# Four score stages of a chunked recurrence in two tensor runs instead of four

## The chip, the cores and the metric

The kernel runs on one core of a Trainium2 chip. The metric is device time in microseconds (us), the median of three executions; beside it stands one profiled execution, whose trace gives the durations below. In the rows, PE is TensorE (PEld its weight loads, PEq its sequencer), DVE is VectorE, ACT is ScalarE, POOL is GpSimd, SP is SyncE, whose queue issues the DMAs here.

## The reference

One layer over 2048 positions of width 1024. One input projection feeds three causal mixers that read the same input; their outputs are gated, concatenated, projected, added to the input and normalized:

```python
h = jnp.einsum('bsd,de->bse', x, w_in)
y_a = _sgu_mixer(a_u, a_v, ...) * silu(a_g)       # A: gMLP, chunks of 128
y_b = _conv_module(b_val, b_glu, ...) * silu(b_g) # B: causal depthwise conv, width 31
y_c = _hgrn2_mixer(c_q, c_f, c_i, lb, ...) * silu(c_g)
y = concat([y_a, y_b, y_c]) @ w_out
return _layernorm(DEEPNORM_ALPHA * x + y, ...)
```

The change is in C, four heads of width 128. With f the forget gate, k = 1 - f, q = silu(c_q) and b the running sum of log f inside a chunk, it needs, for positions t >= s of one chunk,

```python
scores[t, s] = sum_d q[t, d] * k[s, d] * exp(b[t, d] - b[s, d])
o_intra = scores @ v
```

and adds what the state of earlier chunks gives.

## The kernel before, in words

The sequence is worked in two halves of two groups of 512 positions. In each half come branch B, then (first half) A, then the values of C, then C; in the second half A follows C, and the output product ends the program. Each projection (proj_f) is 24 matmuls of 128x512: eight slices of the width, three matmuls each (L201 to L203), since weights and inputs are split into a high part (ACT, L147) and a low part (DVE, L148).

**One unit** of C (hgrn_unit) is one head h on one group g: 16 units. Its PE work is three projections (pm_f, pm_q, pm_cg) and, between their matmuls, short runs of small matmuls. The products of f inside a chunk of 128 are built in levels of 4: T holds the products of f over 1, 4 and 16 positions (T1 is f itself), X the queries and partial queries multiplied by them, K the keys. Four score stages follow each other: stage(0) for pairs inside 4 positions, stage(1) for 16, stage(2) for 64, and chunk_halves for the two halves of 128. Each is one run of matmuls into a bank named sc: 16 of 32x80, 16 of 32x48 (K in pieces of 32 columns), 8 of 64x96 and 4 of 64x64 (pieces of 64 columns). DVE then takes the valid entries over with copy_predicated, into S32 for the first two stages and into ST for the third, and ACT copies S32 onto the diagonal of ST (L433). Behind its matmuls each stage makes the next level: X (L457, L458), T (L469 to L472) and, in place, K (L475, L477); prep (L384 to L389) completes X ahead of a stage.

After the last stage DVE raises K and Q once more (L504, L505), PE transposes K (pk, L515), ACT copies the transposes, PE makes the state increments (pst, L531), DVE chains the states (L539), PE makes the outputs (po, L551 and L555), ACT squares them (jk, L560), POOL takes the inverse root (crs, L228), ACT scales (os, L565), PE transposes back (pt, L573), DVE gates (sg, L575), and SP stores. Branch B's normalization (bt, bb, bhn) runs late and lies partly among the units of C.

**Order.** Every projection slice calls tick(0.64), which advances a clock in the program and emits what is due; later(d, fn) queues a step d units ahead. The delays stand in line 47: stage 0 is due 4.5 after the unit's q projection, the next ones 5.5 after each other, then 2.5, 2.0, 2.5 and 6.0 to transposes, states, outputs and finish. On PE the small runs are pinned to the place in which they are emitted, among the projection matmuls of the same and the next unit. On the other engines a scheduler settles the order when the program is built, and every engine runs its own list strictly in that order.

**Buffers.** X, X4, X16 and Q64 have one buffer each, K and f two; PSUM has 8 banks: three mm for projections, two sc, one each of o (po), st (pst) and tr (pk, pt); B's transposes borrow o, st and tr.

Of the kernel before, what the change touches and what calls it, by code (L numbers as in the profile page):

```python
# [11 lines left out]
F32 = mybir.dt.float32  # L12
# [3 lines left out]
AF = mybir.ActivationFunctionType  # L16
# [30 lines left out]
DST0, DST, DKT, DPST, DPO, DPT = 4.5, 5.5, 2.5, 2.0, 2.5, 6.0  # L47
# [37 lines left out]
def _body(tc, nc, d, ctx):  # L85
# [271 lines left out]
    def hgrn_unit(h, g, gi, w, x, pl, vh, ST, S32):  # L357
        nm = f"{h}_{g}"
        wf_, wq, wg = w
        pf = proj_f(wf_, x, f"f{nm}")  # L360
        f = pl.tile([P, G], F32, tag="f", bufs=2, name=f"f{nm}")
        nc.scalar.activation(f, pf, AF.Sigmoid)
        K = pl.tile([P, G], F32, tag="K", bufs=2, name=f"K{nm}")
        nc.vector.tensor_scalar(f, f, oml[:, h : h + 1], lb[:, h : h + 1], ALU.mult, ALU.add)
        nc.vector.tensor_scalar(K, f, -1.0, 1.0, ALU.mult, ALU.add)

        pq = proj_f(wq, x, f"q{nm}")
        X1 = pl.tile([P, P, 11], F32, tag="X1", bufs=1, name=f"X1{nm}")
        nc.scalar.activation(X1[:, :, 7:11], pq.rearrange("p (n j) -> p n j", j=4), AF.Silu)
        f3 = f.rearrange("p (n j) -> p n j", j=4)  # L370
        nc.vector.tensor_mul(X1[:, :, 0:2], X1[:, :, 7:9], f3[:, :, 0:2])
        nc.vector.tensor_mul(X1[:, :, 4:7:2], X1[:, :, 9:11], f3[:, :, 2:4])

        cur = {"X": X1.rearrange("p n (s b) -> p n s b", b=1), "T": f3}
# [16 lines left out]
        def stage(st):
            b = 4 ** st
            n = G // (4 * b)
            nsc = 10 if st == 0 else 6
            X, T = cur["X"], cur["T"]
            pc = bank("sc", 2, f"sc{nm}_{st}")
            if st < 2:
                npar = 32 // (4 * b)
                w_ = nsc * b * npar
                pcv = pc[:, : 4 * w_].rearrange("p (c w) -> p c w", c=4)  # L400
                for c in range(4):
                    for r in range(4):
                        lo_ = c * P + 32 * r
                        p0 = lo_ // (4 * b)
                        pinned(nc.tensor.matmul(pcv[32 * r : 32 * r + 32, c, :], K[:, lo_ : lo_ + 32],
                                         X[:, p0 : p0 + npar, 1 : 1 + nsc, :],
                                         start=True, stop=True))
# [22 lines left out]
                if st == 1:  # L430
                    for r in range(4):
                        rr = slice(32 * r, 32 * r + 32)
                        nc.scalar.copy(ST[rr, :, rr], S32[rr])  # L433
            else:
                w_ = nsc * b
                pcv = pc[:, : 4 * w_].rearrange("p (c w) -> p c w", c=4)
                for c in range(4):
                    for m in range(2):
                        lo_ = c * P + 64 * m
                        pinned(nc.tensor.matmul(pcv[64 * m : 64 * m + 64, c, :], K[:, lo_ : lo_ + 64],  # L440
                                         X[:, lo_ // 64, 1:7, :], start=True, stop=True))
                for i, (j0, s0, nj) in enumerate(((1, 0, 3), (2, 3, 2), (3, 5, 1))):
                    mo, mw = MOFF[6 + i]
                    for m in range(2):
                        rr = slice(64 * m, 64 * m + 64)
                        nc.vector.copy_predicated(  # L446
                            ST[rr, :, 64 * m + j0 * b : 64 * m + (j0 + nj) * b],
                            msk[rr, mo : mo + mw].unsqueeze(1).to_broadcast([64, 4, mw]),
                            pcv[rr, :, s0 * b : (s0 + nj) * b])

            if st < 2:
                nb = 4 * b
                Xn = pl.tile([P, n // 4, 7, nb], F32, tag=f"X{nb}", bufs=1, name=f"X{nb}_{nm}")
                Xj = X.rearrange("p (m k) s b -> p m k s b", k=4)
                Tj = T.rearrange("p (m k) j -> p m k j", k=4)
                for k0, sl in ((0, slice(0, 2)), (2, slice(4, 7, 2))):
                    nc.vector.tensor_copy(Xn[:, :, sl, 0:b], Xj[:, :, k0 : k0 + 2, 0, :])  # L457
                    nc.vector.tensor_mul(  # L458
                        Xn[:, :, sl, b : 4 * b],
                        Xj[:, :, k0 : k0 + 2, 1:4, :].rearrange("p m k s b -> p m k (s b)"),  # L460
                        Tj[:, :, k0 : k0 + 2, 0:1].to_broadcast([P, n // 4, 2, 3 * b]))
            else:
                Xn = pl.tile([P, n, 64], F32, tag="Q64", bufs=1, name=f"Q64_{nm}")
                nc.vector.tensor_copy(Xn[:, :, 0:b], X[:, :, 0, :])
                nc.vector.tensor_mul(
                    Xn[:, :, b : 4 * b],
                    X[:, :, 1:4, :].rearrange("p n s b -> p n (s b)"),
                    T[:, :, 0:1].to_broadcast([P, n, 3 * b]))
            nc.vector.tensor_mul(T[:, :, 2], T[:, :, 2], T[:, :, 3])  # L469
            nc.vector.tensor_mul(T[:, :, 1], T[:, :, 1], T[:, :, 2])  # L470
            Tn = pl.tile([P, n], F32, tag=f"T{4 * b}", bufs=2, name=f"T{4 * b}_{nm}")
            nc.vector.tensor_mul(Tn, T[:, :, 0], T[:, :, 1])  # L472
# [12 lines left out]
            if st < 2:
                prep(st + 1)
                later(DST, lambda: stage(st + 1))
            else:
                later(DST, chunk_halves)

        def chunk_halves():
            X, T = cur["X"], cur["T"]

            Q = X.rearrange("p (c a) t -> p c a t", a=2)
            K4 = K.rearrange("p (c a t) -> p c a t", a=2, t=64)
            pc = bank("sc", 2, f"sc{nm}_3")
            pcv = pc[:, : 2 * 64].rearrange("p (c w) -> p c w", c=2)
            for c in range(4):
                e = 64 * (c % 2)
                pinned(nc.tensor.matmul(pcv[e : e + 64, c // 2, :], K4[:, c, 0, :], Q[:, c, 1, :],  # L500
                                        start=True, stop=True))
# [3 lines left out]
            nc.vector.tensor_mul(K4[:, :, 0, :], K4[:, :, 0, :], T[:, :, 1:2].to_broadcast([P, 4, 64]))  # L505
# [75 lines left out]
        later(DST0, lambda: stage(0))  # L581
# [211 lines left out]
    def free_c(gi, ft):  # L793
# [75 lines left out]
    stiles.append(pool("stiles", stack=es, side="right"))  # L869
# [181 lines left out]
```

## Time and profile before

| | |
|---|---|
| median of 3 executions | 927.51 us (927.38 to 928.24) |
| the profiled execution's own time | 927.59 us |
| its span, first to last instruction | 925.8 us |
| granted TensorE clock, mean | 0.994 |
| PE busy | 904.1 us (98%) |
| PEld / DVE / ACT / POOL busy | 738.2 / 713.8 / 392.2 / 81.2 us |
| C in the trace, first half | from 200.8 us (first pm_f) |
| first and last score matmul (sc) | 217.2 and 707.1 us |

A group's row gives the source line, engine, operation, out<-in, count, busy time and mean ns of one, then idle time of the engine before them and who ended it. A timeline row gives start and duration in us. The recorded duration of a matmul reaches to its result; the next one starts earlier, so distances between starts, not durations, tell what a matmul costs PE. The trace records two passes for each matmul of C's short runs, so that 16 matmuls read "x32".

### The profile page before, as it was taken

The numbers are of one execution on the slowest core, as the hardware profiler recorded it, in microseconds if no ns is written. First come the engines' busy times: TensorE is split into PE (matmuls) and PEld (weight loads), VectorE is DVE, ScalarE is ACT, GpSimd is POOL, SyncE is SP. The second block draws the span as 40 slices with busy tenths as digits, with TensorE's granted clock in tenths as the row PEclk, the third lists the DMA queues.
The fourth block names the chain that finished last, engine by engine and source line by source line (L and its number), as shares of the span: only waits on it lengthen the run. The fifth ranks groups of instructions, "written<-read, shape, count | busy, mean of one in ns | idle before, by whom it ended". The sixth has DMA issues, their size and how long they took to land.

```text
span 925.8 us, 15037 instructions
## 1 busy us (share of the span) xinstructions
PE 904.1 (98%) x5673; PEld 738.2 (80%) x5673; DVE 713.8 (77%) x1614; ACT 392.2 (42%) x774; POOL 81.2 (9%) x127
## 2 busy tenths in 40 slices
PE   9999998899999999999999999999999999999996
PEld 6889886787777887888888887887889888888885
DVE  5998899935688768997999777778786135898777
ACT  6624355143435336644314334444553343543450
POOL 0001200100010000001000000001012000221122
PEclk9999999899999999999999999999999999999999
DMA  7506786120102103421202011111151498455322
GB/s 259 185 25 224 257 297 248 55 91 24 46 35 69 47 13 110 147 91 64 66 3 92 24 68 36 57 36 58 36 182 58 156 347 292 160 182 183 135 92 91
DMA packets 60808, 107.43 MB, mean 116 GB/s; under 512 B 5312, under 2 KB 21952, under 8 KB 60608
## 3 DMA queue, kind: packets, MB, share of 16 engines
q1 hardware_dynamic: 60736, 106.48, 33.7%
q8 instruction: 44, 0.72, 0.3%
q14 instruction: 28, 0.23, 0.1%
HBM read 75.00 MB, written 31.46 MB: 115 GB/s over the span
## 4 chain that ended last, share of the span: by engine, by line
PE 74%; DVE 13%; DMA 4%; issue 3%; ACT 3%; POOL 2%; SPq 0%; POOLq 0%; DVEq 0%; ACTq 0%
DVE acc L285 5%; PE pm_q L201 3%; PE poz L201 3%; PE poz L203 3%; PE poz L202 3%; PE pm_q L203 3%; PE pm_q L202 3%; PE pm_f L201 3%; PE pm_ci L201 3%; PE pm_ci L203 3%; PE pm_ci L202 3%; PE pm_cg L201 3%; PE pm_f L203 3%; PE pm_f L202 3%; PE pm_cg L202 2%
## 5 line engine op out<-in xcount | busy, mean ns | idle before, releaser
L285 DVE SCALAR_TENSOR_TENSOR acc<-bh,vec,acc 128x512 f32<-128x512 f32 x240 | 172.3, 753 | 2.6
L148 DVE TENSOR_TENSOR wl<-rw,wh 128x512 fp32r<-128x512 f32 x84 | 57.0, 690 | 27.3 <-ACT wh L147 27.1
L147 ACT CAST wh<-rw 128x512 fp32r<-128x512 f32 x84 | 49.9, 618 | 40.7 <-PE pm_f L202 11.1
L201 PE MATMUL pm_f<-xhix,wh 128*128 128x512 f32 x96 | 41.1, 429 | 0.0
L201 PE MATMUL pm_q<-xhix,wh 128*128 128x512 f32 x96 | 40.6, 423 | 0.0
L560 ACT ACTIVATE jk<-po 128x128 f32<-128x128 f32 x64 | 17.7, 277 | 51.9 <-PE po L555 50.9
L201 PE MATMUL pm_cg<-xhix,wh 128*128 128x512 f32 x96 | 39.0, 406 | 0.0
L203 PE MATMUL pm_f<-xhix,wl 128*128 128x512 f32 x96 | 37.7, 393 | 0.0
L202 PE MATMUL pm_q<-xlox,wh 128*128 128x512 f32 x96 | 37.7, 392 | 0.0
L203 PE MATMUL pm_q<-xhix,wl 128*128 128x512 f32 x96 | 37.7, 392 | 0.0
L202 PE MATMUL pm_f<-xlox,wh 128*128 128x512 f32 x96 | 37.6, 392 | 0.0
L203 PE MATMUL pm_cg<-xhix,wl 128*128 128x512 f32 x96 | 37.5, 391 | 0.0
L202 PE MATMUL pm_cg<-xlox,wh 128*128 128x512 f32 x96 | 37.5, 391 | 0.0
L201 PE MATMUL pm_ci<-wh_ci,xhix 128*128 128x512 f32 x96 | 37.4, 389 | 0.0
L203 PE MATMUL pm_ci<-wh_ci,xlox 128*128 128x512 f32 x96 | 37.4, 389 | 0.0
L202 PE MATMUL pm_ci<-wl_ci,xhix 128*128 128x512 f32 x96 | 37.4, 389 | 0.0
L227 POOL TENSOR_SCALAR crs<-ss 128x4 f32<-128x4 f32 x16 | 3.3, 205 | 367.6 <-ACT jk L560 367.6
L355 ACT COPY vh<-pm_ci 128x512 f32<-128x512 f32 x16 | 9.4, 588 | 58.9 <-PE pm_ci L203 58.9
L446 DVE COPY_PREDICATED ST<-msk,sc 64x192 f32<-64x192 int32 (+2 forms) x96 | 28.8, 300 | 5.4 <-PE sc L440 3.1
L503 ACT COPY ST<-sc 64x128 f32<-64x128 f32 x32 | 8.3, 260 | 50.9 <-PE sc L500 50.7
L565 ACT ACTIVATE os<-po,crs 128x128 f32<-128x128 f32 x64 | 18.3, 368 | 24.6 <-POOL crs L228 24.6
L201 PE MATMUL pm_av<-wh_av,xhix 128*128 128x256 f32 x96 | 28.2, 293 | 0.0
(355 smaller groups left out, 2753.1 us busy)
## 6 DMA issues: line engine op xcount, KB each, us to landing
rw<-wf SPq DMA_DIRECT2D x84, 256.0 KB, 3.2
wob<-wo_dr SPq DMA_DIRECT2D x14, 1024.0 KB, 11.5
xr<-x SPq DMA_DIRECT2D x16, 512.0 KB, 3.8
ry<-y_dr SPq DMA_DIRECT2D x32, 256.0 KB, 2.8
out<-xr SPq DMA_DIRECT2D x15, 512.0 KB, 2.6
wo_dr<-wsh SPq DMA_DIRECT2D x28, 256.0 KB, 3.2
wo_dr<-wsl SPq DMA_DIRECT2D x28, 256.0 KB, 2.9
rx<-xT SPq DMA_DIRECT2D x24, 256.0 KB, 3.4
```

What stands on the lines that cost most here:

```text
L147: nc.scalar.copy(hi, src)
L148: nc.vector.tensor_sub(lo, src, hi.bitcast(F32))
L201: nc.tensor.matmul(out, wh, xh, start=first, stop=False, **kw)
L202: nc.tensor.matmul(out, wh, xl, start=False, stop=False, **kw)
L203: nc.tensor.matmul(out, wl, xh, start=False, stop=last, **kw)
L227: nc.gpsimd.tensor_scalar(r, mv_var, scale, EPS, ALU.mult, ALU.add)
L285: nc.vector.scalar_tensor_tensor(a, h[:, k : k + G], vcol(cw + k), a, ALU.mult, ALU.add)
L355: nc.scalar.copy(vh[:, gi * 4 + tt, :], pt)
L446: nc.vector.copy_predicated(ST[rr, :, 64 * m + j0 * b : 64 * m + (j0 + nj) * b], msk[rr, mo : mo + mw].unsqueeze(1).to_broadcast([64, 4, mw]),
L503: nc.scalar.copy(ST[0:64, e:4:2, 64:128], pcv[64 * e : 64 * e + 64])
L560: nc.scalar.activation(jk, po[:, c * P : (c + 1) * P], AF.Square, accum_out=ss[:, c : c + 1])
L565: nc.scalar.mul(os_[:, c * P : (c + 1) * P], po[:, c * P : (c + 1) * P], rs[:, c : c + 1])
```

## The change

**Two runs.** stage(0) and stage(1) become near(): 16 matmuls of 32x80 and 16 of 32x48, back to back, into one bank. stage(2) and chunk_halves become far(): 8 of 64x96 and 4 of 64x64, back to back, into one bank. The matmuls themselves keep their sizes and number.

**Operands ahead.** For the second half of a run to follow the first at once, its operands are made before the run: X4, T4 and the raised keys of level 1 before near(); X16, Q64, T16, T64 and the keys of levels 2 and 3 right behind near()'s matmuls, before far(). The functions raise_x and raise_t hold the old code. The keys of levels 0 and 3 lie in K, those of levels 1 and 2 in a new tile L (one buffer); a new tile D holds two products that were made in place in f. Q64 gets a second buffer. Two copies of a quarter of the keys are added on ACT (K to L and L to K), and the first key raise is split in two on DVE.

**Delays.** near is due 7.0 after the q projection, far 8.0 after near.

**Pools.** The tiles of the output product's sums (ysum) move from a pool of their own into the pool w1.

```diff
-DST0, DST, DKT, DPST, DPO, DPT = 4.5, 5.5, 2.5, 2.0, 2.5, 6.0
+DNEAR, DFAR, DKT, DPST, DPO, DPT = 7.0, 8.0, 2.5, 2.0, 2.5, 6.0
...
-        def stage(st):
+        def raise_x(st):
...
+                Xn = pl.tile([P, n, 64], F32, tag="Q64", bufs=2, name=f"Q64_{nm}")
...
+        def raise_t(st):
+            n = G // (4 * 4 ** st)
+            T = cur["T", st]
+            if st == 0:
+                D = pl.tile([P, n, 2], F32, tag="D", bufs=1, name=f"D{nm}")
+                d1, d2 = D[:, :, 0], D[:, :, 1]
+            else:
+                d1, d2 = T[:, :, 1], T[:, :, 2]
+            nc.vector.tensor_mul(d2, T[:, :, 2], T[:, :, 3])
+            nc.vector.tensor_mul(d1, T[:, :, 1], d2)
...
+            nc.vector.tensor_mul(Tn, T[:, :, 0], d1)
...
+        cur["T", 0] = f3
+        D = raise_t(0)
+        L = pl.tile([P, G], F32, tag="L", bufs=1, name=f"L{nm}")
...
+        nc.scalar.copy(L0[:, :, 3], K0[:, :, 3])
+        nc.vector.tensor_mul(L0[:, :, 0:2], K0[:, :, 0:2], D)
+        nc.vector.tensor_mul(L0[:, :, 2], K0[:, :, 2], f3[:, :, 3])
...
+        def near():
+            pc = bank("sc", 2, f"sc{nm}_0")
+            at = 0
+            for st, Kt, nsc in ((0, K, 10), (1, L, 6)):
...
+                        pinned(nc.tensor.matmul(pcv[32 * r : 32 * r + 32, c, :],
+                                                Kt[:, lo_ : lo_ + 32],
+                                                X[:, p0 : p0 + npar, 1 : 1 + nsc, :],
+                                                start=True, stop=True))
+                cur["pcv", st] = pcv
+            raise_x(1)
+            raise_t(1)
...
+            nc.vector.tensor_mul(L4[:, :, 0:3, :], L4[:, :, 0:3, :],
+                                 T[:, :, 1:4].unsqueeze(3).to_broadcast([P, 32, 3, 4]))
+            prep(2)
+            raise_x(2)
+            raise_t(2)
...
+            nc.scalar.copy(K16[:, :, 3, :], L16[:, :, 3, :])
+            nc.vector.tensor_mul(K16[:, :, 0:3, :], L16[:, :, 0:3, :],
+                                 T[:, :, 1:4].unsqueeze(3).to_broadcast([P, 8, 3, 16]))
...
-                if st == 1:
-                    for r in range(4):
-                        rr = slice(32 * r, 32 * r + 32)
-                        nc.scalar.copy(ST[rr, :, rr], S32[rr])
...
+            for r in range(4):
+                rr = slice(32 * r, 32 * r + 32)
+                nc.scalar.copy(ST[rr, :, rr], S32[rr])
+            later(DFAR, far)
...
-            if st < 2:
-                prep(st + 1)
-                later(DST, lambda: stage(st + 1))
-            else:
-                later(DST, chunk_halves)
...
+        def far():
...
+            for c in range(4):
+                for m in range(2):
+                    lo_ = c * P + 64 * m
+                    pinned(nc.tensor.matmul(pcv[64 * m : 64 * m + 64, c, :], L[:, lo_ : lo_ + 64],
+                                            X[:, lo_ // 64, 1:7, :], start=True, stop=True))
             for c in range(4):
                 e = 64 * (c % 2)
-                pinned(nc.tensor.matmul(pcv[e : e + 64, c // 2, :], K4[:, c, 0, :], Q[:, c, 1, :],
+                pinned(nc.tensor.matmul(pch[e : e + 64, c // 2, :], K4[:, c, 0, :], Q[:, c, 1, :],
                                         start=True, stop=True))
-            for e in range(2):
-                nc.scalar.copy(ST[0:64, e:4:2, 64:128], pcv[64 * e : 64 * e + 64])
+            nc.vector.tensor_mul(K4[:, :, 0, :], K4[:, :, 0, :], T[:, :, 1:2].to_broadcast([P, 4, 64]))
             nc.vector.tensor_mul(Q[:, :, 1, :], Q[:, :, 1, :], T[:, :, 0:1].to_broadcast([P, 4, 64]))
-            nc.vector.tensor_mul(K4[:, :, 0, :], K4[:, :, 0, :], T[:, :, 1:2].to_broadcast([P, 4, 64]))
...
         prep(0)
-        later(DST0, lambda: stage(0))
+        raise_x(0)
+        prep(1)
+        later(DNEAR, near)
...
+            stiles.append(w1)
...
-    stiles.append(pool("stiles", stack=es, side="right"))
```

The rows below show the order on three engines around the unit of head 2 in group 0 (names of its tiles hold 2_0; 2_1 and 3_0 are the next units, 1_1 the one before).

PE before, at stage 0 (the run of stage 1 stands 27 projection matmuls later, alone in the same way):

```order
L203 MATMUL pm_cg2_0_2958<-xhi_first_121,wl_26_0_2771 128x512
L405 MATMUL sc2_0_0_3006<-X12_0_2952,K2_0_2841 32x80 x16
L201 MATMUL pm_f2_1_3041<-xhix1_266,wh_18_0_2750 128x512
L202 MATMUL pm_f2_1_3041<-xlox1_267,wh_18_0_2750 128x512
L203 MATMUL pm_f2_1_3041<-xhix1_266,wl_18_0_2751 128x512
L573 MATMUL pt1_0_3045<-ident_91,os1_0_2944 128x128 x4
```

PE now, at near:

```order
L201 MATMUL pm_f2_1_3074<-xhix1_266,wh_18_0_2780 128x512
L202 MATMUL pm_f2_1_3074<-xlox1_267,wh_18_0_2780 128x512
L203 MATMUL pm_f2_1_3074<-xhix1_266,wl_18_0_2781 128x512
L458 MATMUL sc2_0_0_3084<-X12_0_3014,K2_0_2936 32x80 x16
L458 MATMUL sc2_0_0_3084<-X4_2_0_3020,L2_0_2944 32x48 x16
L201 MATMUL pm_f2_1_3074<-xhix1_266,wh_18_0_2780 128x512
L202 MATMUL pm_f2_1_3074<-xlox1_267,wh_18_0_2780 128x512
L203 MATMUL pm_f2_1_3074<-xhix1_266,wl_18_0_2781 128x512
L585 MATMUL po1_1_3152<-vh_113,ST0_1_1845 128x128
L589 MATMUL po1_1_3152<-s1_0_3_2776,Q64_1_1_2874 128x128
```

The two runs stand together, nine matmuls into the next unit's pm_f, and the outputs po of the unit before follow three matmuls later.

ACT before, from the gate f of unit 3_0 to the scaled outputs os of unit 2_0:

```order
L362 ACT_TABLE_LOAD
L362 ACTIVATE f3_0_3365<-pm_f3_0_3315 128x512
L433 COPY ST0_1_1845<-S320_1847 32x4x32 x4
L560 ACTIVATE jk2_0_0_3450,ss2_0_3449<-po2_0_3441 128x128
L560 ACTIVATE jk2_0_1_3452,ss2_0_3449<-po2_0_3441 128x128
L369 ACT_TABLE_LOAD
L369 ACTIVATE X13_0_3469<-pm_q3_0_3370 128x128x4
L560 ACTIVATE jk2_0_2_3454,ss2_0_3449<-po2_0_3441 128x128
L560 ACTIVATE jk2_0_3_3456,ss2_0_3449<-po2_0_3441 128x128
L565 ACTIVATE os2_0_3461<-po2_0_3441,crs_3458 128x128 x4
```

ACT now:

```order
L594 ACTIVATE jk2_0_0_3438,ss2_0_3437<-po2_0_3429 128x128
L594 ACTIVATE jk2_0_1_3440,ss2_0_3437<-po2_0_3429 128x128
L507 COPY ST0_1_1845<-S320_1847 32x4x32 x4
L594 ACTIVATE jk2_0_2_3442,ss2_0_3437<-po2_0_3429 128x128
L594 ACTIVATE jk2_0_3_3444,ss2_0_3437<-po2_0_3429 128x128
L599 ACTIVATE os2_0_3449<-po2_0_3429,crs_3446 128x128 x4
L422 ACT_TABLE_LOAD
L422 ACTIVATE f3_0_3466<-pm_f3_0_3351 128x512
L438 ACT_TABLE_LOAD
L438 ACTIVATE X13_0_3537<-pm_q3_0_3480 128x128x4
```

The next unit's f stood ahead of the squares jk, the diagonal copies and os; now it stands behind all of them.

DVE before, at the last raise of K of unit 2_0, which the transposes pk read (the next unit's gate, L364, comes twelve rows behind it):

```order
L458 TENSOR_TENSOR X16_2_1_3398<-X4_2_1_3271,T4_2_1_3278 128x8x2x12 x2
L504 TENSOR_TENSOR Q64_2_0_3224<-Q64_2_0_3224,T64_2_0_3229 128x4x64
L505 TENSOR_TENSOR K2_0_2841<-K2_0_2841,T64_2_0_3229 128x4x64
L469 TENSOR_TENSOR T4_2_1_3278<-T4_2_1_3278 128x32
L470 TENSOR_TENSOR T4_2_1_3278<-T4_2_1_3278 128x32
L472 TENSOR_TENSOR T16_2_1_3405<-T4_2_1_3278 128x32
```

DVE now:

```order
L424 TENSOR_SCALAR f2_1_3190<-f2_1_3190,oml_106,lb_105 128x512
L148 TENSOR_TENSOR wl_27_0_3342<-rw27_0_0_3343,wh_27_0_3341 128x512
L425 TENSOR_SCALAR K2_1_3192<-f2_1_3190 128x512
L412 TENSOR_TENSOR D2_1_3195<-f2_1_3190 128x128
L148 TENSOR_TENSOR wl_27_0_3342<-rw27_0_1_3347,wh_27_0_3341 128x512
L413 TENSOR_TENSOR D2_1_3195<-f2_1_3190,D2_1_3195 128x128
L609 SCALAR_TENSOR_TENSOR sg1_1_2778<-pt1_1_3223,vec_96,sg1_1_2778 128x512
L416 TENSOR_TENSOR T4_2_1_3198<-f2_1_3190,D2_1_3195 128x128
L433 TENSOR_TENSOR L2_1_3200<-K2_1_3192,D2_1_3195 128x128x2
L434 TENSOR_TENSOR L2_1_3200<-K2_1_3192,f2_1_3190 128x128
L528 TENSOR_TENSOR K2_0_2936<-K2_0_2936,T64_2_0_3134 128x4x64
```

The raise of K2_0 (L528) now stands behind the next unit's gate f2_1, its key, its products D and T4, its first L, and two low parts of weights (L148).

More of the change, by code (lines that the diff above doesn't have):

```diff
@@ L359, in hgrn_unit @@
         wf_, wq, wg = w
[L360 to L374, printed above, removed]
+        N0 = G // 4
+        cur = {}
         def tb(ap, *shape):
@@ L389, in prep @@
                 nc.vector.tensor_mul(X[:, :, 3, :], X[:, :, 5, :], tb(T[:, :, 1], P, n, b))
-        def stage(st):
+        def raise_x(st):
             b = 4 ** st
             n = G // (4 * b)
-            nsc = 10 if st == 0 else 6
-            X, T = cur["X"], cur["T"]
-            pc = bank("sc", 2, f"sc{nm}_{st}")
+            X, T = cur["X", st], cur["T", st]
             if st < 2:
+                nb = 4 * b
+                Xn = pl.tile([P, n // 4, 7, nb], F32, tag=f"X{nb}", bufs=1, name=f"X{nb}_{nm}")
+                Xj = X.rearrange("p (m k) s b -> p m k s b", k=4)
+                Tj = T.rearrange("p (m k) j -> p m k j", k=4)
+                for k0, sl in ((0, slice(0, 2)), (2, slice(4, 7, 2))):
+                    nc.vector.tensor_copy(Xn[:, :, sl, 0:b], Xj[:, :, k0 : k0 + 2, 0, :])
+                    nc.vector.tensor_mul(
+                        Xn[:, :, sl, b : 4 * b],
+                        Xj[:, :, k0 : k0 + 2, 1:4, :].rearrange("p m k s b -> p m k (s b)"),
+                        Tj[:, :, k0 : k0 + 2, 0:1].to_broadcast([P, n // 4, 2, 3 * b]))
+            else:
+                Xn = pl.tile([P, n, 64], F32, tag="Q64", bufs=2, name=f"Q64_{nm}")
+                nc.vector.tensor_copy(Xn[:, :, 0:b], X[:, :, 0, :])
+                nc.vector.tensor_mul(
+                    Xn[:, :, b : 4 * b],
+                    X[:, :, 1:4, :].rearrange("p n s b -> p n (s b)"),
+                    T[:, :, 0:1].to_broadcast([P, n, 3 * b]))
+            cur["X", st + 1] = Xn
@@ L404, in stage @@
                         p0 = lo_ // (4 * b)
-                        pinned(nc.tensor.matmul(pcv[32 * r : 32 * r + 32, c, :], K[:, lo_ : lo_ + 32],
-                                         X[:, p0 : p0 + npar, 1 : 1 + nsc, :],
-                                         start=True, stop=True))
+                        pinned(nc.tensor.matmul(pcv[32 * r : 32 * r + 32, c, :],
[5 more added lines that the diff above has]
+            raise_t(1)
+            T = cur["T", 1]
+            L4 = L.rearrange("p (n j b) -> p n j b", j=4, b=4)
+            nc.vector.tensor_mul(L4[:, :, 0:3, :], L4[:, :, 0:3, :],
[3 more added lines that the diff above has]
+            raise_t(2)
+            T = cur["T", 2]
+            L16 = L.rearrange("p (n j b) -> p n j b", j=4, b=16)
+            K16 = K.rearrange("p (n j b) -> p n j b", j=4, b=16)
+            nc.scalar.copy(K16[:, :, 3, :], L16[:, :, 3, :])
+            nc.vector.tensor_mul(K16[:, :, 0:3, :], L16[:, :, 0:3, :],
+                                 T[:, :, 1:4].unsqueeze(3).to_broadcast([P, 8, 3, 16]))
+            for st in range(2):
+                pcv = cur["pcv", st]
+                b = 4 ** st
+                nsc = (10, 6)[st]
+                npar = 32 // (4 * b)
                 s5 = S32.rearrange("p c (n j b) -> p c n j b", j=4, b=b)
@@ L451, in stage @@
-            if st < 2:
[L452 to L468, printed above, removed]
@@ new lines, in near @@
+            later(DFAR, far)
+        def far():
+            b = 16
+            pc = bank("sc", 2, f"sc{nm}_2")
+            pcv = pc[:, : 4 * 96].rearrange("p (c w) -> p c w", c=4)
+            pch = pc[:, 4 * 96 :].rearrange("p (c w) -> p c w", c=2)
+            X, T = cur["X", 2], cur["T", 3]
+            Q = cur["X", 3].rearrange("p (c a) t -> p c a t", a=2)
+            K4 = K.rearrange("p (c a t) -> p c a t", a=2, t=64)
+            for c in range(4):
[3 more added lines that the diff above has]
+                                            X[:, lo_ // 64, 1:7, :], start=True, stop=True))
@@ L504, in chunk_halves @@
             nc.vector.tensor_mul(Q[:, :, 1, :], Q[:, :, 1, :], T[:, :, 0:1].to_broadcast([P, 4, 64]))
-            nc.vector.tensor_mul(K4[:, :, 0, :], K4[:, :, 0, :], T[:, :, 1:2].to_broadcast([P, 4, 64]))
             Tc = pl.tile([P, 4], F32, tag="Tc", bufs=2, name=f"Tc{nm}")
             nc.vector.tensor_mul(Tc, T[:, :, 0], T[:, :, 1])
+            for i, (j0, s0, nj) in enumerate(((1, 0, 3), (2, 3, 2), (3, 5, 1))):
+                mo, mw = MOFF[6 + i]
+                for m in range(2):
+                    rr = slice(64 * m, 64 * m + 64)
+                    nc.vector.copy_predicated(
+                        ST[rr, :, 64 * m + j0 * b : 64 * m + (j0 + nj) * b],
+                        msk[rr, mo : mo + mw].unsqueeze(1).to_broadcast([64, 4, mw]),
+                        pcv[rr, :, s0 * b : (s0 + nj) * b])
@@ L508, in chunk_halves @@
+            for e in range(2):
+                nc.scalar.copy(ST[0:64, e:4:2, 64:128], pch[64 * e : 64 * e + 64])
             cur["Q"], cur["Tc"] = Q, Tc
```

65 lines of the change are left out of this document (25 added, 40 removed).

## The prediction

> **What bounds the kernel now.** I read the page's head first, then the waits of PE in the stretch in which C runs, then single runs in the timeline.
>
> ```profile
> span 925.8 us, 15037 instructions
> ...
> PE 904.1 (98%) x5673; PEld 738.2 (80%) x5673; DVE 713.8 (77%) x1614; ACT 392.2 (42%) x774; POOL 81.2 (9%) x127
> ```
>
> PE is busy for 98% of the span, so the time is the length of PE's list: the change can gain by what a run costs PE, and lose by new waits of PE. What PE waits for between 200 and 740 us, the whole of C:
>
> ```profile
> PE pk L515 <- DVE K L505: 2.2, 2, 1.4
> PE bt L316 <- ACT os L565: 1.2, 1, 1.2
> PE pst L531 <- DVE bhn L324: 0.9, 1, 0.9
> PE bb L330 <- DVE sg L575: 0.7, 1, 0.7
> ```
>
> (Columns: total, times, longest.) That is 5.0 us in 16 units. Almost all of C's PE time is work, so I look at what a short run costs. Here are all four, each between the projection matmuls around it (halves, stage 1, stage 2, stage 0):
>
> ```profile
> 540.53 0.39 PE L203 MATMUL pm_f<-xhix,wl 128*128 128x512 f32 x1
> 540.85 0.45 PE L500 MATMUL sc<-Q,K 128*64 128x64 f32 x8
> 541.23 0.50 PE L201 MATMUL pm_f<-xhix,wh 128*128 128x512 f32 x1
> ...
> 545.68 0.40 PE L203 MATMUL pm_q<-xhix,wl 128*128 128x512 f32 x1
> 546.01 0.55 PE L405 MATMUL sc<-X,K 128*32 128x48 f32 x32
> 546.49 0.50 PE L201 MATMUL pm_q<-xhix,wh 128*128 128x512 f32 x1
> ...
> 555.25 0.39 PE L203 MATMUL pm_cg<-xhix,wl 128*128 128x512 f32 x1
> 555.57 0.88 PE L440 MATMUL sc<-X,K 128*64 128x96 f32 x16
> 556.38 0.50 PE L201 MATMUL pm_cg<-xhix,wh 128*128 128x512 f32 x1
> 556.72 0.40 PE L202 MATMUL pm_cg<-xlox,wh 128*128 128x512 f32 x1
> ...
> 560.36 0.39 PE L203 MATMUL pm_cg<-xhix,wl 128*128 128x512 f32 x1
> 560.68 0.76 PE L405 MATMUL sc<-X,K 128*32 128x80 f32 x32
> 561.37 0.50 PE L201 MATMUL pm_f<-xhix,wh 128*128 128x512 f32 x1
> ```
>
> Only distances between starts count. From 556.72 to 560.36 lie 16 projection matmuls: 0.2275 us each. A run's cost is the distance between the projection matmuls around it, less 0.2275, plus what the second matmul behind it is late: 556.38 to 556.72 is 0.34, so 0.11. Halves: 0.70 - 0.2275 + 0.11 = 0.58. Stage 1: 0.81, so 0.69. Stage 2: 1.13, so 1.01. Stage 0: 1.01, so 0.89.
>
> **What joining saves.** Stages 0 and 1 are the same 16 matmuls with 80 and 48 columns: 0.20 us for 32 columns, 0.00625 a column, so the 80 columns are 0.50 and 0.39 is paid once per run, whatever it holds. Stage 2 and the halves, both 64 wide: 8 x 96 = 768 and 4 x 64 = 256 columns, 0.43 us for 512, 0.00084 a column; 768 columns are 0.65, and 0.36 is paid once. The two pairs are of different shape and agree within 0.03. Each unit has two runs fewer: 16 x (0.39 + 0.36) = 12.0. In one unit (head 1 of group 1) the transposes pt stand inside far in the new order and split it: -0.36, leaving **-11.7**. The near run's step from 80 to 48 columns keeps the 32-wide form, far's the 64-wide, so I take the inner join at nothing; bounds -11 to -12.8 from the 0.03 between the pairs on 32 runs.
>
> [...]
>
> **Waits that go.** The 2.2 at pk is replaced by the account below. Of the other three, single meetings of B's steps with C's, I take half: **-3.6** in all (bounds -2.2 and -5.0).
>
> **Edits at nothing.** DVE gets about equal work in another order (one raise of the keys in two pieces, products into D instead of f), and ACT two short copies per unit, 32 in all; neither is the bound. They cost something only where PE comes to wait, through the operands of near, of far, or of pk. Near: from the end of pm_q PE does far, 33 projection matmuls, pk and pst before it, over 33 x 0.2275 + 1.2 = 8.7 us; ACT's gate and some fourteen DVE steps must fit in (durations below: 1.9 + 14 x 0.43 = 7.9). Cover at least 0.8; if it is gone, each unit pays what is over. Far stands 30 and more matmuls and po behind near, over 6.8 us, for a dozen DVE steps of the smaller levels, which the rows below show at 0.4 and less. The moved pool has no wait in it that I can see.
>
> **Where a stall goes.** The orders show one place that gets tight. In the new order ACT runs the next unit's gate f behind the squares of po, the diagonal copies and os, and DVE runs the last raise of K, which pk reads, behind that gate's chain. So between po of one unit and pk of the next there is a loop over ACT, POOL, ACT and DVE that before was not there. ACT's pieces:
>
> ```profile
> 545.33 1.28 ACT L362 ACT_TABLE_LOAD   x1
> 546.62 0.60 ACT L362 ACTIVATE f<-pm_f 128x512 f32<-128x512 f32 x1
> 548.41 1.22 ACT L433 COPY ST<-S 32x128 f32<-32x128 f32 x4 [1.19 <-DVE S L423]
> ...
> 553.62 0.28 ACT L560 ACTIVATE jk<-po 128x128 f32<-128x128 f32 x1 [3.99 <-PE po L555]
> 553.91 0.20 ACT L560 ACTIVATION_READ_ACCUMULATOR jk<-po 128x1 f32 x1
> 554.14 0.28 ACT L560 ACTIVATE jk<-po 128x128 f32<-128x128 f32 x1
> ...
> 558.93 1.14 ACT L565 ACTIVATE os<-po,crs 128x128 f32<-128x128 f32 x4 [1.81 <-POOL crs L228]
> ```
>
> Four squares of 0.52 (553.62 to 554.14), copies 1.22, wait for POOL 1.81, os 1.14, table 1.28, f 0.60: 8.13. DVE's pieces:
>
> ```profile
> 542.39 0.42 DVE L505 TENSOR_TENSOR K<-K,T 128x256 f32<-128x256 f32 x1
> 542.73 0.21 DVE L469 TENSOR_TENSOR T<-T 128x32 f32<-128x32 f32 x1
> 542.86 0.69 DVE L148 TENSOR_TENSOR wl<-rw,wh 128x512 fp32r<-128x512 f32 x1
> 543.46 0.21 DVE L470 TENSOR_TENSOR T<-T 128x32 f32<-128x32 f32 x1
> ...
> 561.95 0.39 DVE L470 TENSOR_TENSOR f<-f 128x128 f32<-128x128 f32 x1
> 562.38 0.40 DVE L472 TENSOR_TENSOR T<-f 128x128 f32<-128x128 f32 x1
> ```
>
> A 512-wide step takes up to 0.60 (542.86 to 543.46), a dependent 128-wide one 0.43, one of 256 0.34, and K's result 0.42. Two 512-wide for f and its key, one for sg of the older unit, counted at 0.5 each since the gate's two need not wait for the full result; three products; two pieces of L at 0.34; K: 1.5 + 1.3 + 0.7 + 0.4 = 3.9. The loop is 12.0. PE meanwhile has, from the end of po to pk, 48 projection matmuls, pt and far: 48 x 0.2275 = 10.9; pt, four matmuls of 128 columns, 0.43 at far's 0.00084 a column; far 1.01 + 0.58 - 0.36 = 1.23; less 0.2 by which po's results come after its slot: 12.4. The **slack is 0.4**, with bounds of +0.8 (each DVE step at its shortest) and -0.2 (a wait at each engine change).
>
> There are 12 such handoffs (units with one before and one after in their half). In seven the new order puts more on DVE ahead of that K: the low parts wl of weights, 0.60 each, and steps of B:
>
> ```profile
> L324 DVE TENSOR_SCALAR bhn<-bt,bmv,brs x16: 534/540/544, 153.0 to 643.7; 128x256 f32<-128x256 f32 x16
> ```
>
> By unit (head, group): (1,0) two bhn and their statistics, for which I take 2.2 (two at 0.54, the statistics before them as long again), and a wl: 2.8 - 0.4 = 2.4; (1,1) one step: 0.2; (2,0) two wl: 0.8; (1,2) and (2,2) three each: 1.4 each; (3,2) four: 2.0; (3,0) has its gate ahead of os, so its pk is on time, but os and pt are then about 0.6 late. Sum **+8.8**; with slack 0.8 about 6, with -0.2 about 14 (every handoff pays then). What is late next: all of PE's list behind pk, by the same amount, so nothing is caught up.
>
> **Sum.** 925.8 - 11.7 - 3.6 + 8.8 = 919.3 of span. The profiled execution's own time, 927.59, is 1.8 above its span and 0.1 from the median of the runs, so the time is **921**.
>
> **The rivals.**
>
> 1. The forecast, 916 to 928 by its bounds (925.8 - 12.8 - 5.0 + 6.0 + 1.8 = 915.8; 925.8 - 11 - 2.2 + 14 + 1.8 = 928.4). Chance 0.56.
>
> 2. No new stall: ACT and DVE finish the loop in time, since the timeline's durations on DVE overlap more than I took. Then 925.8 - 11.7 - 5.0 + 1.8 = 911. For it: the slack without extras is positive, and wl that are ready early could run in DVE's idle time. Against it: DVE goes strictly in order, and the wl stand behind the gate. Chance 0.17.
>
> 3. The other side: the loop po, squares, inverse root, os, f, K, pk closes late in every unit. Its place is ACT, where the diagonal copies now stand among the squares and wait for DVE's copies out of near's bank. The row at 548.41 already waited 1.19 for that; a wait as long in each of the 12 handoffs, on top, gives 921 + 12 x 1.19 = 935. It decides from a mean stall of (11.7 + 3.6) / 12 = 1.28 per handoff; I have 8.8 / 12 = 0.73. For it: near now comes three matmuls ahead of po, not long before. Against: the copies stand behind at least two squares, 1 us after po. Chance 0.13.
>
> 4. The change does not save what it says: the 0.36 to 0.39 are paid wherever the column count or the bank region changes, inside the joined run too. Then 925.8 - 3.6 + 8.8 + 1.8 = 933. Against it: two pairs of other shapes give one price, which fits the border to 128-wide matmuls, and the delay of the matmul behind each run (0.34) lies at that border. Chance 0.05.
>
> 5. [...] Chance 0.05.
>
> The remaining 0.04 is for mishaps at near and far.
>
> **How the numbers follow.** The likeliest is 921. The range 910.5 to 928 takes in the first two cases and the fifth, and leaves out the third, the fourth and the upper rim of the first. A measurement can tell 0.2%, about 1.9 us, from no change. Faster (below 925.6): 0.52 of the first, all of the second, half of the fifth, some of the rest: 0.73. Same: 0.08, from the upper rim of the first and the fifth. Slower: cases three and four and a little: 0.19.
>
> **What would show it.** In the profile after: a joined near from projection matmul to projection matmul as stage 0's 1.01 plus 0.30 for 48 columns; far as stage 2's 1.13 plus about 0.2. If near reads 1.7 instead, case 4 holds. Busy PE should fall by about 12. The waits of PE should show pk behind DVE's K, about seven times, near 8 us, with the longest at (1,0). If pk is absent there, case 2 holds; if it is there 12 times or more at over 1.2, case 3, and the idle time ahead of the diagonal copies on ACT must show it. Waits of sc for X, K or L in many units would mean that I mis-read the cover of near and far; that would make the prediction wrong in a way that none of the cases has.

## The result, and the profile after

The changed kernel takes 938.24 us (median; 938.17 to 941.4) against 927.51 (926.6 to 928.79): a ratio of 1.0128, interval 1.0114 to 1.0141. It is slower; the forecast was 921, faster, and the range ended at 928. The third rival, with 935, lies nearest.

The page of the changed kernel:

```profile
span 939.7 us, 15060 instructions
...
PE 904.6 (96%) x5673; PEld 741.7 (79%) x5673; DVE 716.5 (76%) x1630; ACT 400.4 (43%) x804; POOL 80.6 (9%) x127
```

PE's busy time did not fall by the 12 us that the prediction gave as a sign, though the runs did get cheaper; the account below says where they went. This execution's own time, 941.4, is the longest of the five; the median is 3 us shorter. First the joined runs, far and near, in the timeline (start, duration):

```profile
560.64 0.40 PE L203 MATMUL pm_q<-xhix,wl 128*128 128x512 f32 x1
560.97 0.88 PE L522 MATMUL sc<-X,L 128*64 128x96 f32 x16
561.68 0.40 PE L526 MATMUL sc<-Q,K 128*64 128x64 f32 x8
562.01 0.50 PE L201 MATMUL pm_cg<-xhix,wh 128*128 128x512 f32 x1
...
570.48 0.39 PE L203 MATMUL pm_f<-xhix,wl 128*128 128x512 f32 x1
570.80 0.76 PE L458 MATMUL sc<-X,K 128*32 128x80 f32 x32
571.37 0.52 PE L458 MATMUL sc<-X,L 128*32 128x48 f32 x32
571.83 0.50 PE L201 MATMUL pm_f<-xhix,wh 128*128 128x512 f32 x1
```

By the prediction's reckoning far costs 562.01 - 560.64 - 0.2275 + 0.11 = 1.25 where its two runs cost 1.60, near 1.23 where two cost 1.58 to 1.59. So each join saves 0.35 to 0.36 us.

Then the waits of PE in C, 200 to 750 us (total, times, longest), of which there were 5.0 us before:

```profile
PE pk L549 <- DVE K L528: 5.9, 5, 1.5
PE pt L607 <- ACT bsy L333: 2.9, 2, 1.9
PE po L585 <- DVE T L412: 2.9, 1, 2.9
PE pt L607 <- ACT os L599: 2.7, 1, 2.7
PE pk L549 <- ACT bsy L333: 2.2, 1, 2.2
PE bb L330 <- ACT KT L552: 1.3, 1, 1.3
```

With two small rows they are 18.4 us. One handoff in full, PE first (the last output po of a unit, the last pm_f and pk of the next), then ACT, then DVE:

```profile
574.19 0.39 PE L589 MATMUL po<-s,Q 128*128 128x128 f32 x2
...
576.93 0.39 PE L203 MATMUL pm_f<-xhix,wl 128*128 128x512 f32 x1
...
588.69 0.66 PE L549 MATMUL pk<-ident,K 128*128 128x128 f32 x4 [1.47 <-DVE K L528]
```

```profile
576.77 1.22 ACT L507 COPY ST<-S 32x128 f32<-32x128 f32 x4 [1.34 <-DVE S L498]
578.01 0.28 ACT L594 ACTIVATE jk<-po 128x128 f32<-128x128 f32 x1
...
580.31 1.15 ACT L599 ACTIVATE os<-po,crs 128x128 f32<-128x128 f32 x4 [1.41 <-POOL crs L228]
581.47 1.28 ACT L422 ACT_TABLE_LOAD   x1
582.77 0.60 ACT L422 ACTIVATE f<-pm_f 128x512 f32<-128x512 f32 x1
```

```profile
583.40 0.55 DVE L424 TENSOR_SCALAR f<-f,oml,lb 128x512 f32<-128x512 f32 x1 [6.67 <-ACT f L422]
...
588.23 0.41 DVE L528 TENSOR_TENSOR K<-K,T 128x256 f32<-128x256 f32 x1
```

The gate f waits behind the copies, the last two squares and os, though pm_f's last matmul ended at 577.32, 5.45 us ahead of it; DVE stood idle 6.67 us for it; K's last raise came 4.8 us behind the gate, with three low parts of weights and sg between; and PE waited 1.47 for it. ACT does not catch up between 576.77 and f: 1.34 of waiting for DVE's copies out of near's bank, and 1.41 for POOL's root, lie in the chain.

Last, the granted clock. Windows of the changed kernel (span of the window, its length, busy time of PE, PEld, DVE, ACT and POOL with instructions, then the granted clock as a share of full speed, DMA share, GB/s):

```profile
262.19:265.60 3.41, 2.26 (x69) 1.45 (x67) 3.06 (x12) 0.00 (x0) 0.56 (x2) 1.00 0.00 0
265.60:269.02 3.42, 1.70 (x15) 1.73 (x16) 2.81 (x11) 0.30 (x1) 0.55 (x1) 1.00 0.03 7
371.41:374.83 3.42, 1.41 (x6) 0.96 (x7) 3.42 (x11) 3.35 (x9) 1.53 (x1) 1.00 0.57 190
374.83:378.24 3.41, 3.41 (x27) 2.57 (x27) 2.71 (x6) 3.35 (x6) 0.00 (x0) 0.50 0.51 155
```

```profile
661.50:664.90 3.40, 1.19 (x8) 0.70 (x7) 3.21 (x12) 1.30 (x3) 0.00 (x0) 1.00 0.00 0
664.90:668.30 3.40, 3.40 (x11) 2.62 (x10) 3.33 (x15) 0.48 (x1) 0.00 (x0) 0.51 0.21 77
...
681.90:685.40 3.50, 1.63 (x10) 1.12 (x9) 3.13 (x7) 3.32 (x5) 0.00 (x0) 1.00 0.00 0
685.40:688.80 3.40, 3.40 (x28) 2.58 (x28) 2.83 (x7) 1.92 (x4) 0.00 (x0) 0.51 0.78 242
```

Three times in C PE works for 3.4 us at half clock, each time right behind a long wait (2.70, 2.21 and 1.87 us), and loses 1.7 us by it: 5.1 in all. Projection matmuls start 0.43 us apart there (six steps from 665.10 to 667.66) where they start 0.2275 apart elsewhere. Before, there is none in C: the clock is 1.00 from 200 to 740 us. The two windows over which the wait of 2.87 us that ends at 267.32 is spread (rows one and two) are not followed by one.

### The profile page after: what moved, and what is told of

Same layout as the page of the kernel before. It is cut to its first block, busy times and chain, and to the rows that moved or that the text cites. A ratio compares the mean times of both kernels' runs of the same rounds, so it can differ in the third digit from the quotient of the medians.

```text
span 939.7 us, 15060 instructions
## 1 busy us (share of the span) xinstructions
PE 904.6 (96%) x5673; PEld 741.7 (79%) x5673; DVE 716.5 (76%) x1630; ACT 400.4 (43%) x804; POOL 80.6 (9%) x127
## 5 line engine op out<-in xcount | busy, mean ns | idle before, releaser
L148 DVE TENSOR_TENSOR wl<-rw,wh 128x512 fp32r<-128x512 f32 x84 | 56.6, 687 | 18.7 <-ACT wh L147 18.4
L424 DVE TENSOR_SCALAR f<-f,oml,lb 128x512 f32<-128x512 f32 x16 | 8.7, 544 | 75.3 <-ACT f L422 75.3
L475 ACT COPY K<-L 128x128 f32<-128x128 f32 x16 | 4.8, 299 | 78.4 <-DVE L L467 67.3
```

Source lines behind the costliest of these rows:

```text
L148: nc.vector.tensor_sub(lo, src, hi.bitcast(F32))
L475: nc.scalar.copy(K16[:, :, 3, :], L16[:, :, 3, :])
```

## The experiments

All times are medians; ratios are to the kernel before, measured beside them.

**The joined runs taken apart again.** The second half of near and of far is emitted one projection slice later, and the due times behind it are shortened by as much:

```diff
+            part(0, K, 10)
+            def second():
+                part(1, L, 6)
+                near_rest()
+            later(0.6, second)
...
-            later(DFAR, far)
+            later(DFAR - 0.64, far)
...
+            later(0.6, lambda: far_rest(pcv, pch, Q, K4, T, b))
...
-            later(DKT, transposes)
+            later(DKT - 0.64, transposes)
```

> The changed kernel with each joined run taken apart again by three projection matmuls between its halves; near's second half, far's second half and all that follows them in the code stand one projection slice later, everything else keeps its place. Theory A (joining does save the entry of a run, about 0.36 each, and what was lost is lost in waits elsewhere): 32 entries come back, one of them shared with pt, so 938.2 + 31 x 0.36 = 949 (946 to 952). Rival B (the entry is paid inside the joined run as well, so joining saved nothing): 936 to 940. Rival C (PE waits inside the joined runs for operands of the second half): less than +8, since the second half gets 0.7 us of grace.

Measured: 933.52, ratio 1.0062 (1.0045 to 1.0079): 4.7 *faster* than the joined form. Only C's bound, less than +8, takes that in, and C's mechanism is not there: inside the joined runs PE had waited 0.3 us in all. The runs cost 1.02, 0.59, 0.90 and 0.67 to 0.69 again in its timeline, so the entries did come back, some 11 us. Waits in C and half clock together fell by more:

```profile
PE pk L562 <- DVE K L541: 5.5, 4, 1.9
PE po L598 <- DVE T L412: 1.3, 1, 1.3
PE pt L620 <- ACT bsy L333: 0.9, 1, 0.9
```

The waits are 7.7 instead of 18.4, and half clock costs 1.7 instead of 5.1. On its ACT the diagonal copies stand behind all squares and behind os, in part of the units behind the next f too, where the joined kernel has them among the squares: emitting them one slice later moved them away from where they made os wait. The run does not measure the entries alone, and it made the place of the copies suspect.

**po later.** One number:

```diff
-DNEAR, DFAR, DKT, DPST, DPO, DPT = 7.0, 8.0, 2.5, 2.0, 2.5, 6.0
+DNEAR, DFAR, DKT, DPST, DPO, DPT = 7.0, 8.0, 2.5, 2.0, 8.5, 6.0
```

> The changed kernel with one number changed: the outputs po are due 8.5 instead of 2.5 after the states, so that po of a unit stands behind the last matmul of the next unit's pm_f, as it did before the change. Theory A (the next unit's gate f stands behind po's squares, the diagonal copies and os on ACT, so K, pk and os come late): the waits at pk (9.6 us in the profile, and 0.3 more at the pst behind them) and at pt (7.8) go, and with them the stretches of low granted clock behind long waits (about 5): 913 to 925. Rival D (the waits come from the keys' and queries' raises, which now crowd DVE ahead of near and far, and not from po): pk's waits stay, 933 to 942. Rival E (the waits are mostly steps of branch B that meet C in a shared bank): pk's waits go, those at pt and po stay: 926 to 932.

Measured: 917.32, ratio 0.9887 (0.9871 to 0.9903): 20.9 less than the change, and faster than the kernel before, as theory A had it. ACT now runs f ahead of the squares,

```profile
566.68 1.28 ACT L422 ACT_TABLE_LOAD   x1
567.97 0.60 ACT L422 ACTIVATE f<-pm_f 128x512 f32<-128x512 f32 x1
568.60 1.14 ACT L147 CAST wh<-rw 128x512 fp32r<-128x512 f32 x2
571.26 0.28 ACT L594 ACTIVATE jk<-po 128x128 f32<-128x128 f32 x1 [1.52 <-PE po L589]
```

and the waits in C are 5.2 us in all, the largest

```profile
PE pk L549 <- DVE K L528: 1.6, 3, 0.8
```

with no half clock. Rivals D and E are out: pk's, pt's and po's waits went together, but for 1.8 at pk. (The expectation's 9.6 and 7.8 count by distances between starts; the table has 8.1 at pk and 5.6 at pt.)

**pk and all behind it later.** The same line with DKT 8.5 and DPO 2.5.

> The changed kernel with one number changed: the transposes pk are due 8.5 instead of 2.5 after far, and with them states, outputs and finish; pk, pst, po and pt of a unit then have the places relative to the next unit's projections that they had before the change. Theory A: K's last raise gets four us more, and po stands behind the next pm_f: the waits at pk and pt go, 913 to 925. Rival D (DVE crowded by the raises): pk's waits go here, but not with po alone moved: below 925 here and over 933 there. Rival E: 926 to 932.

Measured: 924.96, ratio 0.9977 (0.9964 to 0.9991). This is the upper end of A's range. pk's waits are gone from its table, as A and D say, but it has 11.1 us of others, among them at pst for ACT's copies KT (2.9), at bt (2.1), at pst for bhn (2.1), at near for T (1.9), and half clock costs 3.4. pk, pst and po now stand close to each other and to near. This run alone would not tell A from D, nor clearly from E; the one before does.

**The diagonal copies on POOL.**

```diff
-                nc.scalar.copy(ST[rr, :, rr], S32[rr])
+                nc.gpsimd.tensor_copy(ST[rr, :, rr], S32[rr])
```

> The changed kernel with the four diagonal copies ST from S32 on POOL instead of ACT, where the squares of po are (they stood between or ahead of them, 1.22 us of copies and up to 1.34 of waiting for DVE's copies out of near's bank); all due times as in the change. Theory A (ACT's loop from po to the next gate f sets the waits): each of some 10 loops is 1.2 to 2.5 shorter, pk's waits (9.6) fall to 0 to 3, pt's (7.8) by about half, and fewer long waits leave fewer stretches of low granted clock: 938.2 falls to 918 to 930. Rival F (the copies stand in time that ACT would wait anyway, for POOL's root or for po): 934 to 940. If POOL runs the copies slowly, crs gets late behind them and the gain is lost: above 934 as well, with os waiting longer for crs than 1.4.

Measured: 929.09, ratio 1.002 (1.0008 to 1.0032): 9.1 less than the change, inside A's range, outside F's. Its waits in C:

```profile
PE pk L549 <- DVE K L528: 3.0, 4, 1.1
PE pt L607 <- ACT bsy L333: 2.8, 2, 1.5
PE pt L607 <- ACT os L599: 2.7, 2, 2.2
```

pk's fell by half and half clock is gone; pt's did not fall, against my expectation. So the copies in ACT's loop are a good part of the loss, and not all of it.

**Four separate runs with early outputs.** The kernel before with its due times alone changed:

```diff
-DST0, DST, DKT, DPST, DPO, DPT = 4.5, 5.5, 2.5, 2.0, 2.5, 6.0
+DST0, DST, DKT, DPST, DPO, DPT = 4.5, 3.1, 3.2, 2.0, 2.5, 6.0
```

> The kernel before, with four separate runs, and due times alone changed (stages due 3.1 instead of 5.5 after each other, pk 3.2 after them), so that the last stage, pk, pst, po and pt stand about where the change has them, po ahead of the end of the next pm_f. Theory A (the place of po is what costs, not the joining): slower than before by what the change lost in waits, 15 to 30, of which the entries are not paid back: 935 to 955; ACT runs f behind os as in the change. Rival G (the loss needs the joined runs and the raises crowded ahead of them): 925 to 932.

Measured: 935.99, ratio 1.0085 (1.0066 to 1.0105), without any joining. PE waits at another place, the last stage:

```profile
PE sc L500 <- DVE K L477: 8.5, 9, 1.6
```

At the longest waits the loop is the same one. ACT, then the DVE step that PE waited for:

```profile
601.82 1.14 ACT L565 ACTIVATE os<-po,crs 128x128 f32<-128x128 f32 x4 [1.41 <-POOL crs L228]
602.98 1.28 ACT L362 ACT_TABLE_LOAD   x1
604.28 0.60 ACT L362 ACTIVATE f<-pm_f 128x512 f32<-128x512 f32 x1
```

```profile
606.75 0.56 DVE L477 TENSOR_TENSOR K<-K,T 128x384 f32<-128x384 f32 x1
```

The gate stands behind os, and the raise of K that the next PE run needs stands behind the gate's steps on DVE. A loss of this kind needs no joining. The run is not clean, though: its stages also stand closer together, and two of the nine waits lie where this loop is not whole. One, 0.67 at 534.66 us, is in the first unit of the second half, which has no outputs of an older unit ahead; one, 1.56 at 707.33, is in the last unit, which has no next gate. How much of the 8.5 comes from the closer stages alone was not told apart.

**pk one slice later, with po late.** Due times 3.3, 1.9, 7.8 and 5.4 behind far.

> The run with po late (917.3), with pk one projection slice later behind far (due 3.3), pst 1.9, po 7.8, and pt 5.4, so that pk, pst and pt stand apart. What is left of waits in C there is 3.1 at pk, 1.4 at the joined pst and pt, 3.3 at bb of B. Theory A: pk's and pst's go, 913 to 916. If the transposes pt now come before os is scaled, a wait at pt of a unit eats that: 917 to 922.

Measured: 916.75, ratio 0.988 (0.9861 to 0.99): the same as with po late, and between the two forecasts. pk's waits for K went, and pt waits for the bank behind KT (2.1) and pk for bsy (1.7) took their place.

**What waits do to the clock.** The kernel before, with this behind pm_q of each unit:

```diff
+        pinned(nc.tensor.transpose(pz[:, 0:P], ident, ident))
+        nc.scalar.copy(Z, pz[:, 0:P])
+        for _ in range(2 * ((probe[0] - 1) % 8)):
+            nc.gpsimd.tensor_scalar(Z, Z, 1.0, 0.0, ALU.mult, ALU.add)
+        pinned(nc.tensor.transpose(pz[:, P : 2 * P], Z, ident))
```

> The kernel before, with a wait made in PE in each of the 16 units behind pm_q: a transpose into a bank, a copy of it on ACT, a chain of 0, 2, ... 14 small POOL operations on the copy (growing over eight units, twice), and a transpose that reads the end of the chain. The waits should be about 1 to 6 us long. If the low granted clock in the changed kernel (0.66 to 0.68 over 5 us behind waits of 2.1 to 3.4) comes from the waits, the long ones of these are followed by such 5 us stretches and the short ones are not, and the time rises by more than the sum of the waits, by about 1.7 for each. If it has another cause, the clock stays at 1.00 behind them.

Measured (one run): 994.87, span 993.2, 67.4 over the span before. The waits, and six us behind the first and the second chain:

```profile
PE pz L588 <- POOL Z L587: 44.5, 14, 5.2
```

```profile
234.50:240.50 6.00, 6.00 (x55) 4.71 (x56) 5.85 (x22) 1.62 (x3) 0.00 (x0) 1.00 0.02 5
260.30:266.30 6.00, 6.00 (x52) 4.73 (x53) 3.47 (x14) 0.79 (x4) 0.00 (x0) 0.78 0.01 3
```

Behind waits of 0.44 and 0.61 us the clock stays at 1.00, and behind one of 2.44, which ends at 595.64; behind the other eleven, of 2.44 to 5.24, it falls. Two of those eleven are 2.44 and 2.45 long, so the length alone does not decide. There are eleven stretches of half clock in C, 47.8 us in all, of which PE works 41.5 and so loses 20.7. With the waits that makes 65.2. The added transposes cost 32 times 0.12, 3.8, by distances between starts, and the other waits in C fell from 5.0 to 1.4: 65.4 of the 67.4. The waits cause the half clock: without them C had none.

**po directly behind the next pm_f.** DPO 4.5.

> The changed kernel with po due 4.5 instead of 2.5 after the states: po of a unit stands directly behind the last matmul of the next pm_f, six matmuls later than in the change and eighteen ahead of its place in the run with po late; ACT's order then has the gate f ahead of po's squares. Theory A in its narrow form (what counts is whether f stands ahead of the squares on ACT, not how late po is): the waits at pk go as in the run with po late, 914 to 921. If po's place matters in itself (a smooth effect of its distance from pk), six of 24 matmuls give about a quarter to a third of the 21 us: 930 to 934.

Measured: 933.12, ratio 1.0063 (1.0046 to 1.008): against theory A's narrow form, and inside the other forecast, 930 to 934. But the waits are not what that forecast supposed. The largest in C:

```profile
PE pk L549 <- DVE sg L609: 13.7, 13, 2.3
```

K was waited for once, 0.6 us, so the loop through f is open as A says; but pt now stands in the bank that pk needs, and sg, which reads pt, stands on DVE behind the next unit's queries. A new wait took the old one's place; the next run takes that one away.

**The same, with pt behind pst.** DPO 4.5, DPT 10.

> The run with po directly behind the next pm_f (933.1), with the transposes pt due 10 instead of 6 after po, so that they stand behind pst, ahead of the next run but one, where the run with po late has them. In that run PE waited 13.7 us at pk for DVE's sg of the unit before, which reads pt out of the bank that pk needs: pt stood 19 matmuls ahead of pk in the same bank, and sg stood on DVE behind the next unit's queries. K itself was waited for only once, 0.6. Theory A with this second loop (pt, sg, bank, pk): its 13.7 go, 933.1 falls to 915 to 921, level with po late (917.3). If po's own place still costs, it stays over 924.

Measured: 922.43, ratio 0.9943 (0.9924 to 0.9962), 10.7 less; just over the range. The 13.7 are gone; pk waits for K by 4.9 in five units, as po late's 1.6 in three did. So po's own place may still count for some of the 5 us between this run and po late; a single cause for them was not shown.

**Entries alone.** The joined runs taken apart as in the first experiment, with DPO 8.5.

> The run with po late (917.3), with both joined runs taken apart again by three projection matmuls, as was done to the changed kernel. There the waits changed with it; here there is little left to change. Joining's own worth: 32 entries of 0.355 come back, 917.3 + 11.4 = 928.7 (926 to 931). If the joined runs save less than their own costs in the timeline say (1.23 and 1.25 against 1.59 and 1.60), below 925.

Measured: 926.54, ratio 0.999 (0.9978 to 1.0001): 9.2 over the run with po late. With little else to move, joining is worth 9 us of time, 11.4 by the runs' own costs; 1.1 of the difference are waits in C, which fell from 5.2 to 4.1. This kernel, four runs' worth of entries and f ahead of po, is level with the kernel before.

**po late, copies on POOL; po in the middle, pt late, copies on POOL.**

> The run with po late, with the diagonal copies on POOL. With f ahead of po the loop is open, so the copies on ACT should cost nothing: theory A expects 915 to 918, the same as with po late, where the same edit took 9 us from the changed kernel. If the copies themselves burden ACT, below 913.

> The same with the diagonal copies on POOL. With po late that edit gave 3.8, where I had expected nothing: there bb's wait for the bank behind KT and one behind bhn became shorter. If the gain is of these meetings on ACT, it comes here too: 911 to 918. If it came from po's place, nothing: as the run without it.

Measured: 913.53, ratio 0.9849 (0.9834 to 0.9864), and 912.47, ratio 0.9846 (0.9829 to 0.9862). The first gained 3.8 where theory A expected nothing: waits in C fell from 5.2 to 3.3, and from the first pm_f to the last pm_ag it takes 546.6 us where po late takes 549.7. The second gained 10.0 and is the fastest here: pk's waits fell from five, 4.9 us, to one of 1.7. How much of it is the copies' time on ACT and how much the order that the scheduler then settles on was not told apart.

## Why the prediction was wrong

**Joining, -11.7: right.** 0.35 to 0.36 per join in the timeline, 32 joins less one: 31 x 0.355 = 11.0; 9.2 as time in the run with the entries alone. Rival 4 falls: near costs 1.23, where it would have 1.58. No run shows a least price of a short matmul, on which the fifth case and its part in the range and the chances rested: near's 1.23 is 0.04 over the 1.19 that stage 0's 0.89 and 48 columns at 0.00625 give.

**Edits at nothing: right.** Near waited 0.3 for X once, far not at all.

**Waits that go, -3.6: right in kind.** pk's row for K is the one that stayed and grew, as the next term has it. Of the other three old rows, 2.8 us, none is among the new; half of that had been taken. Others of the same kind came, under (b).

**Where a stall goes, +8.8: this step failed.** With the term before it, the prediction let waits add 8.8 - 3.6 = 5.2 us; by distances between starts they added 24.4 - 6.2 = 18.2, and half clock 5.1 more. The loop was the right one, as the runs with po late and with the copies on POOL show. The amount for pk came near by luck: 5.9 + 2.2 = 8.1 us in six waits where I had 8.8 in seven. Of the seven handoffs only (1,0), (1,2) and (2,2) waited for K, 0.74, 1.47 and 1.00 where I had 2.4, 1.4 and 1.4. Two more waits for K, 1.49 and 1.17, came at (3,1) and (0,2), the last unit of the first half and the first of the second, which I had not counted at all. The 2.2 is no wait for K but for the bank that B's bsy reads. The two that I had not counted, and ACT ahead of the second:

```profile
405.39 0.66 PE L549 MATMUL pk<-ident,K 128*128 128x128 f32 x4 [1.49 <-DVE K L528]
540.35 0.63 PE L549 MATMUL pk<-ident,K 128*128 128x128 f32 x4 [1.17 <-DVE K L528]
```

```profile
531.48 1.22 ACT L507 COPY ST<-S 32x128 f32<-32x128 f32 x4 [2.01 <-DVE S L498]
532.72 1.28 ACT L422 ACT_TABLE_LOAD   x1
```

At (0,2) no older outputs stand ahead. The diagonal copies waited 2.01 us for DVE, f stood behind them, and DVE had three low parts of weights ahead of K. With the copies on POOL that wait is gone: PE is busy throughout from 537.0 to 555.7 us there.

Wrong was also to price the loop by pk alone, and "nothing is caught up" to be all that follows. Four things were left out. (a) os and B's bsy stand in the same row on ACT, so pt came late too: 5.6 us. I had read pt's lateness into one unit, 0.6. (b) B's transposes borrow the banks of po and pt; one po waited 2.9 for bhn and T, one bb 1.3 for KT: 4.2. (c) The diagonal copies do not only take 1.22 but wait for DVE, 1.34 here. That was the third rival's mechanism, with 0.13: taking them off ACT gave 9.1. The rival's 935 lies near the result, but its sign, pk behind K twelve times at over 1.2, is not there. (d) A wait costs PE more than the table shows. The table counts from the recorded end of the matmul before, 0.39 us after its start, where the next would start 0.2275 after it: the pk at 588.69 shows a wait of 1.47, but by starts it cost 2.13 where an undisturbed one costs 0.44. So the runs of C lost 24.4 us in the profiled execution against 18.4 in the table, and 6.2 against 5.0 before.

**The granted clock, 0: missing from the sum.** Three waits cost another 1.7 each, 5.1.

With these, by starts: 925.8 - 11.0 + 18.2 + 5.1 = 938.1 against a span of 939.7. The landmarks of the two traces agree: C's first pm_f starts at 200.82 before and 200.91 now, from there to the last pm_ag it takes 560.5 and 572.7 us, 12.2 more, where the three terms give 12.3. The remaining 1.6 lie behind C, from the last pm_ag to the last matmul of the output product, 155.0 and 156.6 us. The prediction had no term there, and the cause stays open. PE's busy time is 0.5 us up by the same account: 11.0 less for the joins, 5.1 more for half clock, 4.8 for what waits cost beyond the table, 1.6 behind C.

The weighing of chances erred as the term did: I took a slack of 0.4 us, worked out from one quiet place, for twelve loops whose pieces vary by more than that (in the handoff shown, os waited 1.41 for POOL where I had 1.81, and the copies 1.34 for DVE where I had nothing), and put 0.13 on the case in which they close late.

## What to carry to other kernels

Joining the runs saved their entry here, 0.35 to 0.36 us a join, but with the shorter due times it also shortened the chain behind them and so moved everything that followed, here the outputs, ahead of the next unit's first step on an engine that works its list in order (ACT began f 5.45 us behind its last matmul, after os). After such an edit restore the old distance first, by the due times, and judge the joining then: the same edit was worth +1.3% and -1.1% by one number. When a loop over two engines closes late, follow it past the first wait to all that stands behind on those engines and in the banks that they read, and count what a wait of PE costs beyond itself: three of 1.87 to 2.70 us cost another 1.7 us each at half clock here.

## What the runs showed of the hardware

The three stretches of half clock in the changed kernel last 3.413 us each by the trace's own records, from 374.83, 664.97 and 685.45 us on, at 0.50 of full speed. The waits of PE ahead of them are 2.70, 2.21 and 1.87 us long, and in the rows above PE is busy for 1.41, 1.19 and 1.63 us of the 3.4 to 3.5 us ahead of each. The wait of 2.87 us, the longest, is followed by no such stretch; the two rows over which it is spread have PE busy for 2.26 and 1.70 us. In the run with made waits, one of 2.44 us is followed by half clock and another of 2.44 is not. So in these traces the length of a wait alone does not decide. The four cases in the rows also differ in PE's busy time, 1.63 us and less against 1.70 and more; four cases are too few for a rule, and what decides was not shown.
